# A hybrid encoder step: the small tile moves to the dense expert products, tile 0 to the gathered rows

## Chip, core and metric

The kernel runs on one core of a Trainium2 chip. The metric is the device time of one execution in microseconds; three runs of the kernel before took 3632.94, 3637.1 and 3642.49 us (median 3637.1).

## What is computed

One layer over two streams: a prompt of 1024 frames and a sample of 32 frames with a past of 512. All in float32.

```python
def token_mixer(xn, past_k, past_v, s0, ...):
    z = xn @ w_in                      # 1024 -> 5632
    qa, ka, va, f_pre, q_pre, i_pre, og_pre, gates = jnp.split(z, IN_SPLITS, axis=-1)
    oa = diff_softmax_mix(...)         # 4 heads, two softmax maps, block-causal
    orr, s_new = gla_chunked(...)      # 4 heads, 128x128 state
    y = (jax.nn.sigmoid(ga) * pa + jax.nn.sigmoid(gb) * pb) @ w_out

def peer(xn, w_q, sub_keys, down, up): # 8 heads, 128 x 128 experts of one neuron
    q = (xs @ w_q).reshape(P_TBLOCK, P_HEADS, 2, P_DQ)
    s = jnp.einsum('thcd,hckd->thck', q, sub_keys)
    sv, si = lax.top_k(s, P_TOPK)                      # 16 of 128, twice
    comb = sv[:, :, 0, :, None] + sv[:, :, 1, None, :]
    cv, ci = lax.top_k(comb, P_TOPK)                   # 16 of 256 pairs -> expert e
    gate = jax.nn.softmax(cv, axis=-1)
    hid = jax.nn.gelu(jnp.einsum('thkd,td->thk', down[e], xs), approximate=False)
    return jnp.einsum('thk,thkd->td', gate * hid, up[e])

h = h + token_mixer(rmsnorm(h, norm1))
h = h + peer(rmsnorm(h, norm2))
y = rmsnorm(h, final_norm)
```

Each token uses 8 x 16 = 128 of 16384 experts.

## The kernel before, in words

Tokens lie in nine tiles: 0 to 7 with 128 prompt tokens each, and S with the 32 of the sample. Five generators yield pieces of work with a modelled cost each: `gemm`, `attn`, `routing`, `scatter` and `rows`. A loop at the end of the kernel takes the one that is furthest behind in modelled time; then the framework's scheduler places the instructions on the engines. What results is a fixed order for each engine, and an engine works through its own in order. `issue_after` ties rows and routing to marks of `gemm` (`PACED`).

`gemm` projects the groups of `AG` (`project`), and runs the output stage for the groups of `CDG` (`stage_cd`: gates, w_out, norm, queries, scores). float32 products are three products of split halves (`mm3`). `attn` runs `stage_b` for the groups of `AG`. `routing` finds the 128 experts of a tile (`topk`), in the order `RORDER`.

PEER itself is done in two ways. Tiles in `DENSE` go through all experts: `scatter` writes the gates as a dense matrix to `W_d` with products of one-hot matrices (32 units of four tokens for a full tile, VectorE's `ohB` at line 1138); `hidden(e)` computes gelu of 128 experts for all dense tokens; `gated(e)` multiplies with the gates (line 1217); and `stage_v` multiplies by up-weights and adds into `acc` (line 1280), 32 passes of `jb`, each with four `e`. The tokens are cut into two chunks of `CHUNK` columns. The first `GE` values of `e` are computed before the gates are ready and wait in `early`.

Tiles in `ROWS` gather: for each of a tile's 128 expert places GpSimd issues an indirect DMA of 128 rows of 2048 floats (line 1046), one of three dots is done by GpSimd and ScalarE (1050, 1051) and two by VectorE (1053), ScalarE does gelu and gate (1055, 1056), and VectorE adds the weighted up-row into `xp` (1033). `RB` buffers named `row` turn. Tile S, with 32 tokens, packs four expert places into one gather (32 gathers). A tile's normed input `xg` and its residual `first` come over SP's queue.

Of the kernel before, what the change touches and what calls it, by code (L numbers as in the profile page):

```python
# [9 lines left out]
I32 = mybir.dt.int32  # L10
# [28 lines left out]
RINGS = [(4, 4), (2, 3), (3, 4), (4, 4)]  # L39
SCS = [2, 2, 4, 3]  # L40
# [5 lines left out]
RB, VR, VB, BB, OHB = 5, 3, 2, 4, 4  # L46
# [7 lines left out]
GE = 6  # L54

GC, SC = 1.65, 1.0
# [11 lines left out]
def step_kernel(ctx, tc, x_prompt, x_sample, cache_kT, cache_v, state, norm1, w_in, lam_params,  # L68
# [12 lines left out]
    def open_pool(key, side="left", space=None):  # L81
        kw = dict(space=space) if space is not None else {}
        est[key] = ExitStack()
        P[key] = est[key].enter_context(tc.tile_pool(name=key, bufs=1, side=side, **kw))

# [662 lines left out]
    def stage_cd(ts, rings):  # L748
# [4 lines left out]
        with ExitStack() as st:  # L753
# [99 lines left out]
            def scores(b, qT, keysT):  # L853
                for i, t in enumerate(ts):
# [5 lines left out]
                    pool = P.get("scp") or P.get("oh", wk)  # L860
                    sb = pool.tile([128, 256], F32, name="scs", tag="scs", bufs=SCS[rings])
# [58 lines left out]
    def topk(t):  # L920
        pk, twk = P["pk"], P["twk"]
        T = rows_of(t)
        gate = pk.tile([128, 128], F32, name="gate", tag="gate", bufs=4)
        ei = pk.tile([128, 128], I32, name="ei", tag="ei", bufs=4)
# [3 lines left out]
        if t != "S":  # L928
            ROUTING[t] = (gate, ei)
# [58 lines left out]
        if t == "S":  # L988

            es = pk.tile([128, 32], I32, name="es", tag="es")  # L990
            gs = pk.tile([128, 32], F32, name="gts", tag="gts")
            for g in range(4):
                SP.dma_start(out=es[g * 32:(g + 1) * 32], in_=ei[:32, g * 32:(g + 1) * 32])
                SP.dma_start(out=gs[g * 32:(g + 1) * 32], in_=gate[:32, g * 32:(g + 1) * 32])
            ei, gate = es, gs
        ROUTE[t] = ROUTING[t] = (gate, ei)
# [13 lines left out]
    def rows():  # L1010

        for t in ROWS:
# [3 lines left out]
            T = rows_of(t)  # L1016
            nk = 32 if t == "S" else 128
# [6 lines left out]
            for g in range(128 // T):  # L1024
                SP.dma_start(out=xt[g * T:(g + 1) * T], in_=xn_d[t][:, :])
# [3 lines left out]
            def add(k, row):  # L1029
                if k == 0 and t == "S":  # L1030
                    V.tensor_scalar(acc, row[:, D:], hid[:, 0:1], None, op0=OP.mult)
                else:
                    V.scalar_tensor_tensor(out=acc, in0=row[:, D:], scalar=hid[:, k:k + 1],  # L1033
                                           in1=acc if k else first, op0=OP.mult, op1=OP.add)

            first = None
            if t != "S":
                first = wide("first")[:, 0:D]
                SP.dma_start(out=first, in_=h1_d[t][:, :])

            late = []
            for k in range(nk):
# [15 lines left out]
                yield GC  # L1058
# [3 lines left out]
                yield GC  # L1062
# [3 lines left out]
            sq, fnb, full = hw[:, D:], fw[:, 0:D], fw[:, D:]  # L1066
            SP.dma_start(out=fnb, in_=row_bcast(final_norm))
            ht = acc
            if t == "S":

                ht = hw[:, 0:D]
                SP.dma_start(out=ht[:T], in_=h1_d[t][:, :])
                V.tensor_copy(out=full, in_=acc)
                pw = wide("runs")
                V.tensor_add(ht[:T], ht[:T], acc[:T])
                for g, part in enumerate((pw[:, 0:D], pw[:, D:], sq)):
                    SP.dma_start(out=part[:T], in_=full[(g + 1) * T:(g + 2) * T])
                    V.tensor_add(ht[:T], ht[:T], part[:T])
            normed(gat, ht, fnb, t, sq)
# [3 lines left out]
    NV = 128 * len(DENSE)  # L1083
# [3 lines left out]
    def routing():  # L1087

        for i, t in enumerate(RORDER):
            old = RORDER[i - 4] if i >= 4 else None  # L1090
            while ((t, 0) not in READY or (old in DENSE and old not in DONE)
                   or (t in DEFER and PHASE[0] < 2)):
                yield None
            yield from topk(t)

    def grid(t, s0, q, stg, am, bm):
# [5 lines left out]
        if q + 4 == SB:  # L1102
            o = (128 * DENSE.index(t) + s0) // SB
            SP.dma_start(out=W_d[:, :, o].rearrange("b i j t -> i b j t"), in_=stg)

    def scatter():

        late = None
        for t in [x for ts in CDG for x in ts if x in DENSE]:
# [3 lines left out]
            gate, ei = ROUTE[t]  # L1113
            ij = sct.tile([128, 2, 128], I32, name="ij", tag="ohA", bufs=2)
            V.tensor_scalar(ij[:, 0], ei, 7, None, op0=OP.arith_shift_right)
            V.tensor_scalar(ij[:, 1], ei, 127, None, op0=OP.bitwise_and)
            ijf = sct.tile([128, 2, 128], F32, name="ijf", tag="ohA", bufs=2)
            V.tensor_copy(out=ijf, in_=ij)
            ps = ws_bank()
            for j, src in enumerate((ijf[:, 0], ijf[:, 1], gate)):  # L1120
                PE.transpose(ps[:, j * 128:(j + 1) * 128], src, ident)
            tr = sct.tile([128, 4, 128], F32, name="tr", tag="tr", bufs=1)
            A.activation(tr[:, 0:3], ps.rearrange("p (a t) -> p a t", a=4)[:, 0:3], AF.Copy)
            A.activation(tr[:, 3], ps[:, 0:128], AF.Copy, scale=-1.0)
# [27 lines left out]
    JU, WR = 4, 6  # L1152
# [301 lines left out]
```

## Time and profile before

| | |
|---|---|
| median of three runs | 3637.1 us |
| profiled execution | 3633.46 us |
| its span, first to last instruction | 3631.7 us |
| mean granted TensorE clock | 0.951 |
| TensorE busy | 3261.3 us, 90% |
| VectorE busy | 2795.0 us, 77% |
| ScalarE busy | 1749.2 us, 48% |
| GpSimd busy | 2284.4 us, 63% |

Busy shares are means over stages with different limits, so a table of windows stands among the rows below: its stretches begin where the second attention group's last score products, the output stage's last group, the first gate product, the first product with up-weights, the first accumulate and the 128th accumulate lie. An execution has a fixed part of 1.8 us around the span.

### The profile page before, as it was taken

The page shows a single profiled execution, that of the slowest core. Times are in us where ns is not written, and L with a number is a line of the kernel's source. Part 1 is how long each engine was busy: PE and PEld are TensorE (multiplying, and loading weights), DVE is VectorE, ACT ScalarE, POOL GpSimd, SP SyncE. Part 2 cuts the span into 40 slices and gives each one's busy share as a digit, 9 for nine tenths or more (in the row PEclk, how much of TensorE's full clock was granted, in tenths as well). Part 3 has the DMA queues.
Part 4 walks back from the last instruction along what each step waited for, and adds up shares of the span by engine and source line. Part 5 has one row for each costly group of instructions (what it writes and reads, how often), then busy time and mean ns, then how long its engine had stood idle before and what let it go on. Part 6 is the DMA issues. An engine that isn't in the chain of part 4 may idle for free. (4 is left out here: it accounts for less than half of the span.)

```text
span 3631.7 us, 61063 instructions
## 1 busy us (share of the span) xinstructions
PE 3261.3 (90%) x21635; PEld 3139.3 (86%) x21635; DVE 2795.0 (77%) x5868; ACT 1749.2 (48%) x4314; POOL 2284.4 (63%) x1479
## 2 busy tenths in 40 slices
PE   7999899989898987775888899999999999999997
PEld 7989899878787877775888798999999989999997
DVE  3354468898678989988999998778877788778743
ACT  3544334456777756764443334444444444444432
POOL 2322225546335566686787878888887787888843
PEclk9999999989988999887999999999999999999999
DMA  4554364545555634689788678899988898889842
GB/s 162 166 159 148 118 205 160 161 130 178 177 172 177 216 116 133 204 298 338 283 314 300 247 289 309 331 341 345 335 319 334 308 348 316 327 337 349 321 136 94
DMA packets 357457, 881.05 MB, mean 243 GB/s; under 512 B 31008, under 2 KB 190240, under 8 KB 299808
## 3 DMA queue, kind: packets, MB, share of 16 engines
q1 hardware_dynamic: 297248, 440.91, 36.5%
q0 software_dynamic: 59904, 436.23, 32.2%
q8 instruction: 171, 2.80, 0.3%
q14 instruction: 134, 1.10, 0.1%
HBM read 784.47 MB, written 92.14 MB: 241 GB/s over the span
## 5 line engine op out<-in xcount | busy, mean ns | idle before, releaser
L263 PE MATMUL gv<-vwh,uh 128*128 128x320 f32 x2048 | 644.0, 315 | 105.1 <-DVE acc L1280 67.8
L257 POOL TENSOR_TENSOR wl<-wr,wh 128x1024 fp32r<-128x1024 f32 x160 | 390.4, 2453 | 542.9 <-ACT wh L256 501.9
L263 PE MATMUL gv<-vxh,dh 128*128 128x320 f32 x2048 | 646.1, 316 | 43.7 <-DVE acc L1280 31.1
L265 PE MATMUL gv<-vxh,dl 128*128 128x320 f32 x2048 | 639.9, 314 | 7.3 <-POOL dl L257 7.3
L264 PE MATMUL gv<-vxl,dh 128*128 128x320 f32 x2048 | 641.7, 314 | 0.0
L265 PE MATMUL gv<-vwh,ul 128*128 128x320 f32 x2048 | 635.7, 312 | 4.0 <-POOL ul L257 4.0
L264 PE MATMUL gv<-vwl,uh 128*128 128x320 f32 x2048 | 638.6, 312 | 0.0
L1046 POOL DMA_INDIRECT row<-in_p_rows_dram,ei x384 | 490.6, 1278 | 194.2 <-DVE xp L1033 90.2
L1033 DVE SCALAR_TENSOR_TENSOR xp<-row,hid,xp 128x1024 f32<-128x1024 f32 x412 | 528.1, 1282 | 85.7 <-ACT hid L1056 77.2
L1053 DVE CUSTOM_DVE_ANT_0 row<-row,xg 128x1024 f32<-128x1024 f32 x276 | 507.3, 1838 | 9.3 <-DMA row<-in_p_rows_dram,ei 9.3
L263 PEld LDWEIGHTS gv<-vwh,uh 128*128 128x128 f32 x2048 | 389.0, 190 | 117.9 <-DVE acc L1280 78.5
L263 PEld LDWEIGHTS gv<-vxh,dh 128*128 128x128 f32 x2048 | 394.3, 193 | 50.3 <-issue 32.3
L257 POOL TENSOR_TENSOR ul<-ur,uh 128x512 fp32r<-128x512 f32 x256 | 349.9, 1371 | 131.8 <-ACT uh L256 100.2
L265 PEld LDWEIGHTS gv<-vxh,dl 128*128 128x128 f32 x2048 | 392.5, 192 | 8.6 <-POOL dl L257 8.5
L264 PEld LDWEIGHTS gv<-vxl,dh 128*128 128x128 f32 x2048 | 394.2, 193 | 0.0
L265 PEld LDWEIGHTS gv<-vwh,ul 128*128 128x128 f32 x2048 | 389.1, 190 | 5.1 <-POOL ul L257 5.1
L257 POOL TENSOR_TENSOR dl<-dr,dh 128x512 fp32r<-128x512 f32 x256 | 338.0, 1328 | 86.7 <-ACT dh L256 68.6
L264 PEld LDWEIGHTS gv<-vwl,uh 128*128 128x128 f32 x2048 | 390.0, 190 | 0.0
L1141 POOL TENSOR_TENSOR ohB<-ohB,tr 128x512 f32<-128x512 f32 x160 | 195.4, 1227 | 255.5 <-DVE ohB L1138 216.3
L1050 POOL TENSOR_TENSOR row<-row,xg 128x1024 f32<-128x1024 f32 x140 | 342.3, 2445 | 3.5 <-DMA row<-in_p_rows_dram,ei 2.7
L1280 DVE TENSOR_TENSOR acc<-acc,gv 128x320 f32<-128x320 f32 x496 | 235.3, 480 | 135.9 <-PE gv L265 132.8
L256 ACT ACTIVATE uh<-ur 128x512 fp32r<-128x512 f32 x256 | 160.5, 629 | 231.6 <-PE gv L264 173.0
(327 smaller groups left out, 7812.2 us busy)
## 6 DMA issues: line engine op xcount, KB each, us to landing
dr<-in_p_downT_dram SPq DMA_DIRECT2D x256, 256.0 KB
ur<-in_p_up_dram SPq DMA_DIRECT2D x256, 256.0 KB
wr<-in_w_in_dram SPq DMA_DIRECT2D x88, 512.0 KB
W_d<-stg SPq DMA_DIRECT2D x40, 1024.0 KB
gw<-W_d SPq DMA_DIRECT2D x32, 1280.0 KB
wr<-in_p_wq_dram SPq DMA_DIRECT2D x48, 512.0 KB
wr<-in_w_out_dram SPq DMA_DIRECT2D x24, 512.0 KB
wr<-in_w_a_dram SPq DMA_DIRECT2D x12, 512.0 KB
```

Of the source, the lines that this page charges most:

```text
L256: A.activation(h, src, AF.Copy)
L257: (lo_engine or G).tensor_tensor(out=l, in0=src, in1=h.bitcast(F32), op=OP.subtract)
L263: PE.matmul(out, lh, rh, start=(i == 0), stop=False)
L264: PE.matmul(out, lh, rl, start=False, stop=False)
L265: PE.matmul(out, ll, rh, start=False, stop=(i == n - 1))
L1033: V.scalar_tensor_tensor(out=acc, in0=row[:, D:], scalar=hid[:, k:k + 1], in1=acc if k else first, op0=OP.mult, op1=OP.add)
L1046: G.indirect_dma_start(out=row, out_offset=None, in_=p_rows, in_offset=bass.IndirectOffsetOnAxis(ap=ei[:, k:k + 1], axis=0))
L1050: G.tensor_tensor(out=row[:, 0:D], in0=row[:, 0:D], in1=xt, op=OP.mult)
L1053: V.tensor_tensor_reduce(out=row[:, 0:D], in0=row[:, 0:D], in1=xt, scale=1.0, scalar=0.0, op0=OP.mult, op1=OP.add, accum_out=h)
L1141: G.tensor_tensor(out=bm, in0=bm, op=OP.mult, in1=tr[:, 2, xs].unsqueeze(2).to_broadcast([128, 4, 128]))
L1280: V.tensor_add(acc[:, db, cs], acc[:, db, cs], ps[:, :CHUNK])
```

## The change

S joins the first projection group, the second output group and the dense tiles; tile 0 leaves the dense tiles and is gathered first. A dense tile may now have 32 tokens, so widths come from `VT` and offsets from `VO`. NV falls from 640 to 544. Gathers become 4 x 128 = 512 instead of 3 x 128 + 32 = 416; the packing of four places for S goes. The pools of the gather open at the end of the second attention group instead of at `v_start`; `gemm` waits for that end before the second output group instead of before the third. While `PHASE` is 0 a gather counts 6.6 us of modelled time instead of 3.3. There are four `row` buffers instead of five, eight early values of `e` instead of six, eight buffers for the gated values instead of six, and the scatter's one-hot tiles no longer have a pool of their own with four buffers.

```diff
-AG = [[0, 1, 2, 3, 4], [5, 6, 7, "S"]]
-CDG = [[0, 1, 2], [3, 4], [5, 6, 7, "S"]]
-DENSE = [0, 1, 2, 3, 4]
-ROWS = [5, 6, "S", 7]
-RORDER = [0, 1, 2, 3, 4, 5, 6, 7, "S"]
+AG = [[0, 1, 2, 3, 4, "S"], [5, 6, 7]]
+CDG = [[0, 1, 2], [3, 4, "S"], [5, 6, 7]]
+DENSE = [1, 2, 3, 4, "S"]
+ROWS = [0, 5, 6, 7]
+RORDER = [0, 1, 2, 3, 4, "S", 5, 6, 7]
...
-RINGS = [(4, 4), (2, 3), (3, 4), (4, 4)]
-SCS = [2, 2, 4, 3]
+RINGS = [(4, 4), (2, 3), (3, 3), (4, 4)]
+SCS = [2, 2, 2, 3]
...
+KEPT = dict(d=4, r=3)
-RB, VR, VB, BB, OHB = 5, 3, 2, 4, 4
+RB, VR, VB, BB = 4, 3, 2, 4
-GE = 6
-GC, SC = 1.65, 1.0
+GE = 8
+GC, SC = (3.3, 1.65, 1.65), 1.0
...
-            for k in range(nk):
+            for k in range(128):
...
-                yield GC
+                yield GC[PHASE[0]]
...
-    NV = 128 * len(DENSE)
+    VT = [rows_of(t) for t in DENSE]
+    VO = [sum(VT[:i]) for i in range(len(VT))]
+    NV = sum(VT)
...
-        for i, t in enumerate(RORDER):
-            old = RORDER[i - 4] if i >= 4 else None
-            while ((t, 0) not in READY or (old in DENSE and old not in DONE)
+        for t in RORDER:
+            ts, n = (DENSE, KEPT["d"]) if t in DENSE else (ROWS, KEPT["r"])
+            old = ts[:max(0, ts.index(t) + 1 - n)]
+            while ((t, 0) not in READY or not all(x in DONE for x in old)
...
-            for s0 in range(0, 128, SB):
+            for s0 in range(0, T, SB):
...
-                    pool, bufs = (P["oh"], OHB) if "oh" in P else (sct, 2)
-                    am, bm = [pool.tile([128, 4, 128], F32, name=x, tag=x, bufs=bufs)
+                    am, bm = [sct.tile([128, 4, 128], F32, name=x, tag=x, bufs=2)
...
-    JU, WR = 4, 6
+    JU, WR = 4, 8
...
             ring.close()
+            yield from until("B1")
             with tc.tile_pool(name="scp", bufs=1) as P["scp"]:
...
-            open_pool("oh")
-            yield from until("B1")
             rings("right")
...
-        for key in ("gw", "va", "vk", "vx", "gat"):
+        for key in ("gw", "va", "vk", "vx"):
             open_pool(key, side="right")
-        open_pool("xgp", space=PS)
...
                 yield from stage_b(i)
+            if i == len(AG) - 1 and stop != "mixer":
+
+                open_pool("gat", side="right")
+                open_pool("xgp", side="right", space=PS)
             STATE.add("B%d" % i)
```

How that moves instructions shows at three places. The first is VectorE's order near the end of the dense products, before: `xp` is the sum of a gathered tile, `acc` that of the dense tiles, `msf` the start of a gathered tile's last norm.

```order
L257 TENSOR_TENSOR vwl<-gv,vwh 128x320
L1033 SCALAR_TENSOR_TENSOR xp<-row,hid,xp 128x1024
L1217 TENSOR_TENSOR gv<-gv,gw 128x320
L1033 SCALAR_TENSOR_TENSOR xp<-row,hid,xp 128x1024
L257 TENSOR_TENSOR vwl<-gv,vwh 128x320
L1280 TENSOR_TENSOR acc<-acc,gv 128x320
L240 TENSOR_SCALAR msf<-ssf 128x1
```

The last two row-adds of the last gathered tile stand there, and 48 accumulates and the last gates still follow them. The same engine in the changed kernel, at its last accumulates (`first` is the residual with which a tile's first row-add begins, `ht` the dense tiles' residual):

```order
L1262 TENSOR_TENSOR acc<-acc,gv 128x272
L1024 SCALAR_TENSOR_TENSOR xp<-row,hid,first 128x1024
L1262 TENSOR_TENSOR acc<-acc,gv 128x272
L1224 TENSOR_TENSOR ht<-ht,gv 128x512 x2
L1224 TENSOR_TENSOR ht<-ht,gv 32x512
L1262 TENSOR_TENSOR acc<-acc,gv 128x272 x2
L1042 ISA row,hid<-row,xg 128x1024
L1042 ISA hid 128x1
L1262 TENSOR_TENSOR acc<-acc,gv 128x272 x2
```

Here stands the first row-add of the last gathered tile; 385 of 512 row-adds are placed up to the last accumulate, and 127 after it.

The second place is SP's queue around the load of tile 7's `xg` (`xn_119` is its normed input, `ur` an up-block of the dense products). Before:

```order
L1268 DMA ur<-in_p_up_dram 128x512
L1164 DMA dr<-in_p_downT_dram 128x512
L1268 DMA ur<-in_p_up_dram 128x512
L1025 DMA xg<-xn_119 128x1024
L1164 DMA dr<-in_p_downT_dram 128x512
L1268 DMA ur<-in_p_up_dram 128x512
```

And in the changed kernel:

```order
L1246 DMA fnb<-in_final_norm_dram 128x1024
L1250 DMA ur<-in_p_up_dram 128x512
L1056 DMA fnb<-in_final_norm_dram 128x1024
L1250 DMA ur<-in_p_up_dram 128x512 x2
L1019 DMA xg<-xn_119 128x1024
L1250 DMA ur<-in_p_up_dram 128x512 x2
L1028 DMA first<-h_7_108 128x1024
```

96 up-blocks stood behind that load, and 2 do now.

The third place is TensorE's order at the attention's end (`gb` is an attention product, `ws` one of the scatter, `gm<-act` one of the output stage). Before:

```order
L265 MATMUL gm<-act,wl 128x256
L263 MATMUL gm<-act,wh 128x256
L264 MATMUL gm<-act,wh 128x256
L858 MATMUL gm<-keysT,qT 128x128 x2
L530 MATMUL gb<-ident,on 128x32 x4
L265 MATMUL gm<-act,wl 128x256
```

And in the changed kernel:

```order
L679 MATMUL gb<-ident,kk 128x128 x4
L1081 MATMUL ws<-ohB,ohA 128x128 x4
L685 MATMUL gb<-iv,kkn 128x128 x4
L1081 MATMUL ws<-ohB,ohA 128x128 x8
L536 MATMUL gb<-ident,on 128x128 x4
L1081 MATMUL ws<-ohB,ohA 128x128 x20
L269 MATMUL gm<-act,wh 128x288
```

The attention's last transposes stood among products of the second output group; now that group's first product stands behind them.

## Rows read from the trace of the kernel before

**Rows 1.** the page, engines (instructions) and GB/s moved in 40 slices
```profile
PE 3261.3 (90%) x21635; PEld 3139.3 (86%) x21635; DVE 2795.0 (77%) x5868; ACT 1749.2 (48%) x4314; POOL 2284.4 (63%) x1479
...
GB/s 162 166 159 148 118 205 160 161 130 178 177 172 177 216 116 133 204 298 338 283 314 300 247 289 309 331 341 345 335 319 334 308 348 316 327 337 349 321 136 94
```

**Rows 2.** stretch, us; busy us PE, PEld, DVE, ACT, POOL; clock, DMA share, GB/s
```profile
998.00:1234.00 236.00, 207.56 (x1509) 188.31 (x1510) 191.16 (x535) 176.24 (x447) 108.62 (x68) 0.89 0.61 190
1234.00:1554.00 320.00, 261.99 (x1653) 248.35 (x1653) 301.33 (x844) 205.48 (x495) 188.61 (x117) 0.90 0.49 159
1554.00:1678.00 124.00, 62.03 (x378) 59.50 (x376) 97.50 (x106) 71.51 (x201) 95.24 (x65) 0.72 0.91 331
1678.00:1742.00 64.00, 58.60 (x374) 57.55 (x375) 61.63 (x173) 29.38 (x78) 50.49 (x34) 0.95 0.84 293
1742.00:2278.00 536.00, 467.39 (x2991) 459.21 (x2990) 507.53 (x982) 212.02 (x543) 431.04 (x289) 0.94 0.80 292
2278.00:3611.00 1333.00, 1286.72 (x8664) 1276.73 (x8664) 982.18 (x1391) 562.42 (x1439) 1033.30 (x714) 0.99 0.83 305
3611.00:3632.00 21.00, 1.85 (x17) 1.62 (x15) 11.86 (x24) 3.17 (x10) 6.16 (x5) 0.62 0.32 125
```

**Rows 3.** the same view for the accumulates, line 1280
```profile
2278.00:3611.00 1333.00, 176.09 (x369) 0.99 0.83 305
```

**Rows 4.** the same view for the row-adds, line 1033
```profile
1554.00:1678.00 124.00, 36.27 (x29) 0.72 0.91 331
...
2278.00:3611.00 1333.00, 341.44 (x266) 0.99 0.83 305
3611.00:3632.00 21.00, 0.00 (x0) 0.62 0.32 125
```

**Rows 5.** timeline of TensorE at 320 columns: start, duration, instruction
```profile
2400.31 0.31 PE L265 MATMUL gv<-vxh,dl 128*128 128x320 f32 x1
...
2401.48 0.31 PE L264 MATMUL gv<-vxl,dh 128*128 128x320 f32 x1
```

**Rows 6.** the same view at 256 columns
```profile
60.02 0.28 PE L265 MATMUL gm<-wh,xl 128*128 128x256 f32 x1
...
60.74 0.28 PE L265 MATMUL gm<-wh,xl 128*128 128x256 f32 x1
```

**Rows 7.** groups by line: count | busy us, mean ns | idle before, releasers
```profile
L1033 DVE SCALAR_TENSOR_TENSOR xp<-row,hid,xp 128x1024 f32<-128x1024 f32 x412 | 528.1, 1282 | 85.7 <-ACT hid L1056 77.2 <-issue 2.7 <-ACT hid L1055 2.4
L1053 DVE CUSTOM_DVE_ANT_0 row<-row,xg 128x1024 f32<-128x1024 f32 x276 | 507.3, 1838 | 9.3 <-DMA row<-in_p_rows_dram,ei 9.3
L1046 POOL DMA_INDIRECT row<-in_p_rows_dram,ei x384 | 490.6, 1278 | 194.2 <-DVE xp L1033 90.2 <-issue 31.6 <-DVE si L906 8.1
...
L257 POOL TENSOR_TENSOR ul<-ur,uh 128x512 fp32r<-128x512 f32 x256 | 349.9, 1371 | 131.8 <-ACT uh L256 100.2 <-ACT hid L1055 19.2 <-ACT hid L1056 5.5
L1050 POOL TENSOR_TENSOR row<-row,xg 128x1024 f32<-128x1024 f32 x140 | 342.3, 2445 | 3.5 <-DMA row<-in_p_rows_dram,ei 2.7
L257 POOL TENSOR_TENSOR dl<-dr,dh 128x512 fp32r<-128x512 f32 x256 | 338.0, 1328 | 86.7 <-ACT dh L256 68.6 <-ACT hid L1055 10.3 <-PE gv L265 2.0
...
L969 DVE TENSOR_TENSOR oh<-cf,iota_c 128x800 f32<-128x800 f32 (+1 forms) x72 | 100.1, 1391 | 0.8
...
L974 DVE TENSOR_REDUCE ef<-oh 128x16 f32<-128x800 f32 (+1 forms) x72 | 70.0, 973 | 16.2 <-POOL oh L972 16.2
...
L1053 DVE DVE_READ_ACCUMULATOR2_ANT hid<- 128x1 f32 x276 | 21.6, 78 | 0.0
```

**Rows 8.** busy time by stretch of the scatter's one-hot products, line 1138
```profile
1234.00:1554.00 320.00, 57.42 (x60) 0.90 0.49 159
```

**Rows 9.** the page, GpSimd's DMA queue: packets, MB, share of 16 engines
```profile
q0 software_dynamic: 59904, 436.23, 32.2%
```

**Rows 10.** VectorE's dots, line 1053: min/median/max ns, first and last start
```profile
L1053 DVE CUSTOM_DVE_ANT_0 row<-row,xg x276: 1194/1306/5851, 1533.9 to 3462.4; 128x1024 f32<-128x1024 f32 x138
```

**Rows 11.** waits: who for whom, us in total, times, longest
```profile
POOL row L1046 <- DVE xp L1033: 93.3, 71, 5.6
```

More of the change, by code (lines that the diff above doesn't have):

```diff
@@ L922, in topk @@
         T = rows_of(t)
-        gate = pk.tile([128, 128], F32, name="gate", tag="gate", bufs=4)
-        ei = pk.tile([128, 128], I32, name="ei", tag="ei", bufs=4)
+        kind = "d" if t in DENSE else "r"
+        gate = pk.tile([128, 128], F32, name="gate", tag="gate" + kind, bufs=KEPT[kind])
+        ei = pk.tile([128, 128], I32, name="ei", tag="ei" + kind, bufs=KEPT[kind])
         g3 = gate.rearrange("p (h r) -> p h r", h=PH)
@@ L927, in topk @@
         hg = HG.get(t, PH)
-        if t != "S":
-            ROUTING[t] = (gate, ei)
+        ROUTING[t] = (gate, ei)
         for h0 in range(0, PH, hg):
@@ L987, in topk @@
             yield 1.0
[L988 to L996, printed above, removed]
+        ROUTE[t] = (gate, ei)
         yield 3.0
@@ L1023, in rows @@
             xt = gat.tile([128, D], F32, name="xg", tag="xg", bufs=1)
-            for g in range(128 // T):
-                SP.dma_start(out=xt[g * T:(g + 1) * T], in_=xn_d[t][:, :])
+            SP.dma_start(out=xt, in_=xn_d[t][:, :])
             hid = gat.tile([128, 128], F32, name="hid", tag="hid", bufs=1)
@@ L1029, in add @@
             def add(k, row):
[L1030 to L1039, printed above, removed]
+                V.scalar_tensor_tensor(out=acc, in0=row[:, D:], scalar=hid[:, k:k + 1],
+                                       in1=acc if k else first, op0=OP.mult, op1=OP.add)
+            first = wide("first")[:, 0:D]
+            SP.dma_start(out=first, in_=h1_d[t][:, :])
             late = []
-            for k in range(nk):
+            for k in range(128):
                 while t not in ROUTE and HEADS.get(t, 0) * 16 <= k:
@@ L1065, in rows @@
             hw, fw = wide("ht"), wide("fnb")
-            sq, fnb, full = hw[:, D:], fw[:, 0:D], fw[:, D:]
+            sq, fnb = hw[:, D:], fw[:, 0:D]
             SP.dma_start(out=fnb, in_=row_bcast(final_norm))
[L1068 to L1079, printed above, removed]
+            normed(gat, acc, fnb, t, sq)
+            DONE.add(t)
             yield 4.0
-    NV = 128 * len(DENSE)
+    VT = [rows_of(t) for t in DENSE]
+    VO = [sum(VT[:i]) for i in range(len(VT))]
+    NV = sum(VT)
     SB = 16
@@ L1237, in residual @@
                 cs = slice(d0 * 128, d0 * 128 + 512)
[L1238 removed]
+                for i, (o, T) in enumerate(zip(VO, VT)):
                     ps = gv_bank()
                     for d in range(4):
[L1241 to L1246 removed]
+                        PE.transpose(ps[:T, d * 128:(d + 1) * 128], acc[:, d0 + d, o:o + T], ident)
+                    V.tensor_add(ht[:T, i, cs], ht[:T, i, cs], ps[:T])
+                    A.activation(sq[:T, i, cs], ht[:T, i, cs], AF.Square,
+                                 accum_out=s2[:T, d0 // 4, i:i + 1])
+                    G.tensor_tensor(out=ht[:T, i, cs], in0=ht[:T, i, cs], in1=fnb[:T, cs], op=OP.mult)
             for jb in range(NJ):
@@ L1254, in stage_v @@
                     ss = wk.tile([128, len(DENSE)], F32, name="ss", tag="ss", bufs=1)
[L1255 removed]
+                    V.memset(s2, 1.0)
+                    late = [(ht[:VT[i], i], h1_d[t][:, :]) for i, t in enumerate(DENSE)]
                     late.append((fnb, row_bcast(final_norm)))
@@ L1345, in gemm @@
             yield None
-        for key in ("oh", "sct", "mc"):
+        for key in ("sct", "mc"):
             est[key].close()
@@ L1393, in step_kernel @@
         blocked.clear()
-    for key in ("xgp", "gat", "vx", "vk", "va", "gw", "twk", "pk"):
+    for key in ("xgp", "vx", "vk", "va", "gw", "gat", "twk", "pk"):
         est[key].close()
```

47 lines of the change are left out of this document (21 added, 26 removed).

## The prediction, made before the changed kernel had run

> **What bounds the kernel now.** I read the engine shares first, then busy time by stage, then the spacing of single matmuls, then the groups of VectorE and GpSimd. TensorE is busy 90% of the span [rows 1], but by stage there are two regimes [rows 2]. [...] From 1742 to 2278 us VectorE is busy 507.5 of 536 us: it is the bound, and the first eight passes of the dense products (a pass is one value of `jb`, 16 accumulates) take 67 us each. From 2278 to 3611 us TensorE is the bound: 23 passes (368 accumulates) in 1333 us, 57.96 us each [rows 3]. All 416 gathers are over before the dense products are: the last of the 415 row-adds falls in the stretch that ends at 3611 us, none follows [rows 4], and only 21 us of closing work stand behind the last accumulate.
>
> A matmul of 320 columns starts every 0.146 us (eight steps from 2400.31 to 2401.48) and one of 256 every 0.120 us (six steps from 60.02 to 60.74) [rows 5, 6]. A pass is 384 matmuls of 320 columns, 56.2 us of pure spacing, so it runs at 1.032 of it.
>
> **Dense products.** NV falls from 640 to 544, a chunk from 320 to 272 columns, counts stay. Between the two spacings 272 columns cost 0.120 + 16/64 x 0.026 = 0.1266 us. A pass becomes 384 x 0.1266 = 48.6 us, x 1.032 = 50.2 us. POOL could hold it: in the order 9.9 gathers stand in a pass (228 row-adds over 23 passes; before 266, 11.6 each), so 9.9 x (1.278 + 0.337 x 2.445) + 8 x 1.328 + 8 x 1.371 = 42.4 us [rows 7], 83% of it against 78% before; I add 0.7 us. The 23 passes take 23 x 50.9 = 1170 us, **-163 us**. Ends: 23 x 48.6 (-215) and 57.96 kept (0); I stay near the ratio of the row.
>
> First eight passes: in the order VectorE has 28 row-adds fewer between accumulates 1 and 128 (77 against 105) at 1.282 + 2/3 x 1.916 = 2.56 us (-72 us), 46 us less routing (tile 6's is ahead of it now), and 9 us less from narrower gates and accumulates. Its 507.5 us become 380, at the same 95% 400 us. TensorE asks 8 x 50.2 = 402 us. Two engines at the limit take turns badly, so 425 us instead of 536, **-111 us** (ends -136 and -40).
>
> **Up to the first accumulate.** Tile 0's gathers now stand among routing and scatter. Ahead of its first accumulate VectorE's order has 80 row-adds instead of 44 (36 x 1.282 = +46 us), 54 dots instead of 30 (24 x 1.916 = +46 us), 136 one-hot products instead of 160 (24 x 0.957 = -23 us) [rows 7, 8], and routing for six heads more, some 27 us (their two one-hot steps alone are 6 x (1.391 + 0.973) = 14 us). That is +96 us on an engine busy 88% of 744 us. Also, the attention's end is now waited for ahead of the second group of the output stage: in TensorE's order 172 attention matmuls and 119 of the scatter stand alone, where before nearly all of the attention's last 305 lay among the output stage's (a stretch of TensorE's order only; what they take alone no row shows). Dense work queues behind it. If VectorE stays 88% busy the first accumulate is 96/0.88 = 109 us later; if its 92 us of idle time take up the gathers, 0; if the lone attention adds idle time like the 45 of 236 us that VectorE has there now [rows 2], or somewhat more, 170. I take **+105 us**: where gathers meet routing VectorE is busy 94 to 96% [rows 2], so there is little left to fill.
>
> Moved edits that I cost at nothing: S goes from the second projection group to the first (columns 640 + 416 become 672 + 384, three chunks both times); its outputs come from the dense stage instead of regrouped gathers (32 gathers less, which are in the counts above); eight gelu columns instead of six wait ahead of the gates, hidden beside the scatter as now. If that cover is gone, two columns are 96 matmuls, 12 us.
>
> **The tail.** Here the order decides. In VectorE's order 415 of 415 row-adds stood ahead of the last accumulates; now 385 of 512 do, and 127 follow, all of tile 7. SP's queue loads tile 7's `xg` with two up-blocks left behind it, where 96 were left before, so no dot of it can start earlier. Nothing is left beside them: each gather of 128 rows x 8 KiB = 1.049 MB is exposed. Price of one: GpSimd's queue moved 436.23 MB in 32.2% of sixteen engines' span, 436.23/(0.322 x 3631.7 us) = 373 GB/s, 2.81 us [rows 9]. VectorE alone, at the dot's median 1.306 us [rows 10]: 1.282 + 2/3 x (1.306 + 0.077) = 2.20 us. Above: 29 row-adds in the 124 us from 1554 to 1678 [rows 4], 4.3 us, with scatter, weights and hidden columns beside them. I take 3.0 us, near the queue's price, since four buffers keep the transfers back to back: 127 x 3.0 = 381 us (279 to 546). Behind the last add stands one norm and one store, some 13 us, instead of the 21 us of now: **+373 us**.
>
> [...]
>
> **Sum.** The profiled execution took 3633.46 us (span 3631.7). 3633.5 + 105 - 111 - 163 + 373 = 3837.5 us. The median of the runs is 3.6 us above that execution: 3840 us.
>
> **Rivals.**
> *The scatter sets the start (other side).* The gates wait for the last scatter unit; 24 units fewer at 320/60 = 5.3 us each [rows 8] would bring the dense start 128 us forward instead of 105 back: 3837 - 233 = 3604 us. For it: 92 us of idle VectorE there. Against: VectorE works in order and has 96 us more. It decides only if the first accumulate comes before about 1650 us. 4%.
> *VectorE paces the tail.* 127 x 2.20 = 279 us: 3735 us. Against: the queue's price is above that. 12%.
> *The tail is latency.* With four buffers instead of five each gather waits for its predecessor's add: 4.3 us, 546 us: 4003 us. For it: GpSimd waited 93.3 us for row-adds [rows 11]. 10%.
> *Passes don't shorten.* GpSimd's splits queue behind gathers that wait for one of four buffers, a pass stays 57.96 us: 3837 + 163 = 4000 us. Against: POOL's 42 us fit in 50. 8%.
> *The change doesn't do what it says* can be read off: tile 0 does start early (59 of its row-adds ahead of the first gate), yet the dense end is reached with 385 done where the earlier start was to leave fewer. That is in the forecast.
>
> **Chances.** Forecast 66%, its own range 3760 to 3920 us. Range for 8 in 10: 3700 to 3960 us, which takes in VectorE's tail and leaves out most of the three others. Under 0.3% (11 us) this kernel's runs can't tell from none. Faster 4% (the scatter rival), same 2% (a mixture of it with a fast tail), slower 94%.
>
> **What would show it.** Right: TensorE idle for the last 350 to 420 us, with row-adds as VectorE's main work and one queue at some 350 GB/s; last accumulate near 3445 us; first near 1847 us; passes near 51 us; TensorE's low share also between attention's end and the second group's first product. Wrong: row-adds of tile 7 beside dense matmuls; a last accumulate above 3550 us or a first below 1742 us; a gather above 3.6 us in the tail.

## The result, and the profile after

The changed kernel takes 3908.3 us (median of 4 runs, 3899.4 to 3909.2) against 3636.4 us of the kernel before: ratio 1.074, 95% interval 1.0719 to 1.0762. The forecast was 3840 us, its range 3700 to 3960 us. Line numbers are now those of the changed kernel: row-add L1024, dot L1042, gather L1035, accumulate L1262.

The page of the changed kernel, answering to [rows 1, 9]: the engines' busy time, TensorE's busy tenths and granted clock in 40 slices, GpSimd's DMA queue.

```profile
PE 3039.0 (78%) x21443; PEld 2908.2 (74%) x21443; DVE 2904.9 (74%) x6064; ACT 1759.4 (45%) x4428; POOL 2443.5 (63%) x1583
...
PE   7999979998756568767788999999999999960000
...
PEclk9999989989878679878899999999999999985555
...
q0 software_dynamic: 73728, 536.90, 36.7%
```

TensorE has nothing to do in the last four slices, and the queue carries 100.7 MB more: the 96 added gathers. The stages, in the columns of [rows 2]:

```profile
990.00:1133.00 143.00, 89.93 (x516) 74.77 (x514) 76.07 (x169) 96.22 (x263) 40.04 (x35) 0.77 0.50 156
1133.00:1306.00 173.00, 105.71 (x674) 97.74 (x674) 135.29 (x153) 90.24 (x234) 103.44 (x68) 0.80 0.81 280
1306.00:1538.00 232.00, 165.92 (x985) 155.65 (x985) 220.09 (x723) 86.71 (x173) 129.99 (x66) 0.82 0.63 225
1538.00:1758.00 220.00, 152.24 (x889) 144.12 (x889) 198.78 (x554) 146.57 (x358) 143.50 (x89) 0.83 0.44 139
1758.00:1887.00 129.00, 89.53 (x603) 84.76 (x601) 83.04 (x90) 89.50 (x245) 83.12 (x63) 0.80 0.69 233
1887.00:1939.00 52.00, 45.65 (x310) 44.26 (x311) 48.96 (x141) 21.23 (x60) 30.95 (x24) 0.88 0.81 292
1939.00:2378.00 439.00, 397.41 (x3025) 392.36 (x3025) 409.06 (x832) 181.81 (x467) 353.26 (x245) 0.96 0.79 285
2378.00:3490.00 1112.00, 1091.11 (x8605) 1085.65 (x8603) 855.71 (x1289) 510.11 (x1330) 954.36 (x667) 0.99 0.89 328
3490.00:3897.00 407.00, 1.23 (x10) 0.78 (x8) 272.61 (x318) 112.33 (x350) 266.25 (x171) 0.50 0.86 324
```

From 990 us (last projection matmul) to 1133 us (the second output group's first product) TensorE is busy 63%, all of it attention and scatter. The first accumulate starts at 1939 us, the last at 3490 us, and 407 us without TensorE follow. The same view for the row-adds alone:

```profile
3490.00:3897.00 407.00, 162.49 (x127) 0.50 0.86 324
```

The 127 row-adds stand in the tail as the order said, 407/127 = 3.2 us each. Span against span the 275 us divide as follows, in us:

| part | before | after | measured | forecast |
|---|---|---|---|---|
| start to first accumulate | 1742 | 1939 | +197 | +105 |
| first eight passes | 536 | 439 | -97 | -111 |
| 23 later passes | 1333 | 1112 | -221 | -163 |
| behind the last accumulate | 21 | 417 | +396 | +373 |

A piece of the tail's timeline (start, duration, engine, line; in brackets the idle time before and who ended it):

```profile
3703.74 0.94 POOL L1035 DMA_INDIRECT row<-in_p_rows_dram,ei  x1 [1.19 <-DVE xp L1024]
3704.77 1.22 DVE L1042 CUSTOM_DVE_ANT_0 row<-row,xg 128x1024 f32<-128x1024 f32 x1
...
3706.59 1.29 DVE L1024 SCALAR_TENSOR_TENSOR xp<-row,hid,xp 128x1024 f32<-128x1024 f32 x1 [0.60 <-ACT hid L1045]
...
3710.87 1.23 DVE L1042 CUSTOM_DVE_ANT_0 row<-row,xg 128x1024 f32<-128x1024 f32 x1 [2.99 <-DMA row<-in_p_rows_dram,ei]
...
3713.57 0.95 POOL L1035 DMA_INDIRECT row<-in_p_rows_dram,ei  x1 [2.93 <-DVE xp L1024]
```

Two waits face each other: VectorE's dot waits 2.99 us for a row to land, and GpSimd's next gather waits 1.19 to 2.93 us for a row-add to free a buffer. Which of them sets the 3.2 us, the timeline can't say.

### The profile page after: what moved, and what is told of

The parts are those of the page before. It is cut to its first block, busy times and chain, and to the rows that moved or that the text cites. A ratio compares the mean times of both kernels' runs of the same rounds, so it can differ in the third digit from the quotient of the medians.

```text
span 3906.7 us, 61161 instructions
## 1 busy us (share of the span) xinstructions
PE 3039.0 (78%) x21443; PEld 2908.2 (74%) x21443; DVE 2904.9 (74%) x6064; ACT 1759.4 (45%) x4428; POOL 2443.5 (63%) x1583
## 4 chain that ended last, share of the span: by engine, by line
PE 36%; DVE 24%; POOL 8%; issue 7%; DMA 7%; ACT 4%; POOLq 0%; SPq 0%; DVEq 0%; ACTq 0%
PE gv L271 9%; PE gv L269 9%; PE gv L270 8%; DVE xp L1024 5%; POOL row L1039 3%; DMA row<-in_p_rows_dram,ei 3%; DVE row L1042 3%; POOL row L1035 3%; PE gm L270 2%; PE gm L269 2%; PE gm L271 2%; PE ws L1081 2%; DVE oh L974 1%; DVE ohB L1120 1%; ACT row L1040 1%
## 5 line engine op out<-in xcount | busy, mean ns | idle before, releaser
L1035 POOL DMA_INDIRECT row<-in_p_rows_dram,ei x512 | 652.5, 1274 | 322.2 <-DVE xp L1024 184.6
L1024 DVE SCALAR_TENSOR_TENSOR xp<-row,hid,xp 128x1024 f32<-128x1024 f32 x508 | 652.1, 1284 | 133.1 <-ACT hid L1045 121.1
L1042 DVE CUSTOM_DVE_ANT_0 row<-row,xg 128x1024 f32<-128x1024 f32 x340 | 582.7, 1714 | 128.6 <-DMA row<-in_p_rows_dram,ei 128.3
L269 PE MATMUL gv<-vxh,dh 128*128 128x272 f32 x2048 | 598.4, 293 | 45.9 <-DVE vwl L263 20.2
L269 PE MATMUL gv<-vwh,uh 128*128 128x272 f32 x2048 | 593.8, 290 | 23.9 <-DMA ur<-in_p_up_dram 12.5
L271 PE MATMUL gv<-vxh,dl 128*128 128x272 f32 x2048 | 596.6, 294 | 13.7 <-POOL dl L263 13.4
L270 PE MATMUL gv<-vxl,dh 128*128 128x272 f32 x2048 | 595.7, 292 | 0.0
L271 PE MATMUL gv<-vwh,ul 128*128 128x272 f32 x2048 | 589.4, 290 | 4.9 <-POOL ul L263 4.8
L270 PE MATMUL gv<-vwl,uh 128*128 128x272 f32 x2048 | 592.7, 290 | 0.0
L1044 ACT ACTIVATE hid<-hid 128x1 f32<-128x1 f32 x512 | 100.5, 198 | 573.5 <-DVE hid L1042 566.8
L1040 ACT ACTIVATE row<-row 128x1024 f32<-128x1024 f32 x172 | 181.9, 1057 | 315.2 <-POOL row L1039 312.3
```

What stands on the lines that cost most here:

```text
L269: PE.matmul(out, lh, rh, start=(i == 0), stop=False)
L270: PE.matmul(out, lh, rl, start=False, stop=False)
L271: PE.matmul(out, ll, rh, start=False, stop=(i == n - 1))
L1035: G.indirect_dma_start(out=row, out_offset=None, in_=p_rows, in_offset=bass.IndirectOffsetOnAxis(ap=ei[:, k:k + 1], axis=0))
L1040: A.activation(row[:, 0:D], row[:, 0:D], AF.Copy, accum_out=h)
L1042: V.tensor_tensor_reduce(out=row[:, 0:D], in0=row[:, 0:D], in1=xt, scale=1.0, scalar=0.0, op0=OP.mult, op1=OP.add, accum_out=h)
```

## The experiments

A time below is that of a single run unless an interval stands beside it.

### The start: lone attention or gathers

First the kernel before, in which the loop that orders the work issues the second output group behind the attention's last TensorE instruction:

```diff
+            yield from until("B1")
+            CDF[0] = 1
+            yield 0.0
             with tc.tile_pool(name="scp", bufs=1) as P["scp"]:
...
+        if x[0] == "gemm" and CDF[0] and tails:
+            hold = tails[-1]
```

> The kernel before, whole and with its own tiles and gathers, with one edit: the second output group's instructions are issued only behind the attention's last TensorE instruction, so that 190 attention and 115 scatter matmuls stand alone ahead of it in TensorE's order (172 and 119 in the changed kernel, 13 and 16 in the kernel before). Theory (the lone attention is part of the late start): the 123 us that the changed kernel's trace shows between the last projection matmul and the second group's first product, less what still overlaps, come back here: first accumulate 80 to 130 us later than 1742 us, total 3715 to 3765 us. Rival (VectorE's added gathers alone make the start late, and the attention only changes places): first accumulate within 30 us of 1742 us, total 3630 to 3665 us.

The first accumulate came at 1829 us, 87 us later, and the run took 3732.6 us against 3648.7 us of the kernel before beside it. Its stretch from the last projection matmul to the attention's end:

```profile
979.00:1120.00 141.00, 108.91 (x537) 80.58 (x537) 83.48 (x208) 97.84 (x293) 36.91 (x30) 0.67 0.46 135
```

141 us, as the changed kernel's 143 (the 123 us of the expectation are a misreading); VectorE is busy 59% of them. The theory holds: the lone attention alone is worth 84 to 87 us in the kernel before.

Then both kernels without the gathers but each tile's first:

```diff
+                if k and True:
+                    yield GC[PHASE[0]]
+                    yield GC[PHASE[0]]
+                    continue
                 row = wide("row")
```

> The changed kernel without 127 of the 128 gathers of each of tiles 0, 5, 6 and 7 (508 of 512, with their dots and row-adds; the output of these four tiles is left incomplete); every other instruction keeps its place. Theory: 79 of them stood ahead of the first accumulate, 79 x 2.56 us of VectorE at its 88% there is 230 us, so the first accumulate comes near 1710 us; what is left above the same kernel before without gathers is the lone attention. The tail vanishes: nothing but closing work of some 20 us behind the last accumulate. TensorE holds the passes at 47 to 48.5 us in both dense stretches, total 1710 + 31 x 47.7 + 20 = 3210 us. Rival 1 (the lone attention and the scatter make all of the late start, the gathers lay in idle time): first accumulate at 1850 us or later. Rival 2 (gathers, not TensorE, pace the passes even late): passes below 46 us.

> The kernel before without the gathers but the first of each of its tiles 5, 6, 7 and S (412 of 416 left out with their dots and row-adds; these tiles' output is left incomplete). The partner of the run above: the first accumulate should come 43 x 2.56 / 0.88 = 125 us sooner, near 1617 us; passes stay near 57.5 us, in the first eight too, total 1617 + 31 x 57.6 + 21 = 3424 us. The two first accumulates' distance is what the change adds ahead of the dense work without gathers: the theory of the lone attention gives 80 to 130 us, the theory that gathers alone explain the +197 us gives under 30 us.

The dense stages, of the changed kernel without gathers and then of the kernel before without them (first accumulate to accumulate 128, and to the last):

```profile
1775.00:2152.00 377.00, 375.11 (x2983) 374.19 (x2982) 193.94 (x619) 130.40 (x263) 190.29 (x141) 1.00 0.37 123
2152.00:3239.00 1087.00, 1087.00 (x8668) 1086.95 (x8667) 327.29 (x758) 361.00 (x727) 473.16 (x364) 1.00 0.35 115
```

```profile
1674.00:2131.00 457.00, 447.21 (x3007) 444.15 (x3006) 220.46 (x676) 135.93 (x264) 200.54 (x146) 0.99 0.32 105
2131.00:3420.00 1289.00, 1274.92 (x8658) 1268.17 (x8657) 368.10 (x777) 365.40 (x729) 472.77 (x364) 1.00 0.31 100
```

The first accumulates are 1775 and 1674 us, 101 us apart without a gather. So of the +197 us the new structure ahead of the dense work makes 101 and the gathers 96. Of the 101, the lone attention accounts for 87 if it costs here what it cost in the kernel before; 10 already lie ahead of the last projection matmul, which comes at 991 us against 981. The gathers cost 164 us for 79 now and 68 us for 43 before. A gather there costs 2.1 and 1.6 us, less than the 2.9 us I had put into both expectations, which is why both first accumulates come 57 to 65 us later than I wrote. TensorE alone needs 1087/23 = 47.3 us for a pass, and 48.3 us with gathers: it is the bound there, as forecast.

The two whole runs say what the change is worth by itself: 3264.7 us against 3442.9 us, so without gathers the changed kernel is 178 us the faster one. Its 508 left-out gathers, with their dots and row-adds, cost 644 us; the 412 of the kernel before cost 194 us.

### The tail: who sets 3.2 us

The changed kernel with tile 7's places cut into stretches:

```diff
+                m = 64 if t == 7 and k >= 80 else 128
...
+                if t == 7 and (56 <= k < 80 or k >= 104):
+                    A.activation(h, gate[:m, k:k + 1], AF.Copy)
+                elif k % RP == 1 and not (t == 7 and 32 <= k < 56):
```

> The changed kernel with tile 7's 128 places cut in five stretches: places 0 to 31 as they are; 32 to 55 with all dots on VectorE and none on GpSimd; 56 to 79 with no dot at all, only the row-add (the dots are left out); 80 to 103 as they are but with 64 rows in each gather instead of 128; 104 to 127 with 64 rows and no dots (tile 7's output is left wrong). Spacing of row-adds in the five, us each. Theory (the transfers' bytes pace the tail): 3.2, 3.2, 3.2, then 1.6 to 2.2 (VectorE's own work takes over), then 1.6; total some 60 us below 3907 us. Rival 1 (each gather's latency over four buffers): 3.2, 3.2, about 3.0, 2.9 to 3.2, 2.9, total within 25 us of 3907 us. Rival 2 (GpSimd's queue, in which a gather is issued behind a multiply that waits for its row): 3.2, 2.7, below 2.5, 3.0, below 2.0. Rival 3 (VectorE paces): 3.2, then 2.7 to 3.2, then 1.3.

Row-adds (VectorE's busy time and their count) from one row-add's start to another's, well inside each of the five stretches; then clock, DMA share, GB/s:

```profile
3499.90:3590.53 90.63, 33.42 (x26) 0.50 0.90 333
3608.34:3666.01 57.67, 23.18 (x18) 0.50 0.92 341
3679.21:3724.84 45.63, 23.18 (x18) 0.50 1.01 421
3747.52:3812.24 64.72, 23.03 (x18) 0.50 0.68 146
3826.56:3875.51 48.95, 24.32 (x19) 0.50 1.02 206
```

Width by count: 3.49, 3.20, 2.54, 3.60 and 2.58 us; the run took 3887.2 us. None of the four theories fits. With all dots on VectorE the pace is 3.20 us, and the changed kernel takes 3.22 us at those places, so the multiplies on GpSimd don't set it. Without dots the sixteen DMA engines are full (share 1.01) and a gather takes 2.5 us; half the rows take as long. So I split the question anew: a fixed latency over the buffers, or a full queue, and ran two kernels on it, one with more row buffers and one with fewer (the last two lines of the diff are the second kernel's).

```diff
+                    open_pool("tl")
+                if t == 7 and k >= 32 and (k < 80 or k % 5 > 1):
+                    row = P["tl"].tile([128, 2 * D], F32, name="row", tag="row", bufs=6)
...
-RB, VR, VB, BB = 4, 3, 2, 4
+RB, VR, VB, BB = 3, 3, 2, 4
```

> The changed kernel; tile 7's places 0 to 31 gather into the four row buffers as they are, from place 32 on into a second pool of six buffers (opened when the dense stage has left its memory), from place 80 on into both in turn, ten buffers. Places 64 to 79 and 104 to 127 have no dot, only the row-add (tile 7's output is left wrong by those). Spacing of the row-adds, us each, for 4 buffers, 6 with dots, 6 without, 10 with, 10 without. Theory A (a gather takes some 8.6 us from issue to use whatever its bytes, as the equal 2.49 and 2.56 us for 128 and 64 rows suggest, so four buffers set the pace): 3.2 to 3.5, 2.3 to 2.7, 1.7, 2.2 to 2.4 (VectorE's own work), 1.3; total 3775 to 3810 us. Theory B (the queue carries 421 GB/s and is full, so bytes set the floor and buffers don't matter): 3.2 to 3.5, 2.7 to 3.2, 2.5, 2.5 to 3.0, 2.5; total 3840 to 3880 us.

> The same five stretches of tile 7 as in the run with stretches before (as is; all dots on VectorE; no dots; 64 rows; 64 rows and no dots, the output of tile 7 left wrong), but with three row buffers instead of four in the whole kernel; 141 row-adds instead of 127 stand behind the last accumulate. Theory A (latency over the buffers): 4.2 to 4.7, 4.0, (8.6 + 1.5) / 3 = 3.4, 4.2 to 4.8, 3.4. Theory B (bytes): as with four, 3.5, 3.0, 2.5, at most 3.6, 2.5. The dense passes beside fewer gathers stay within 1 us of 48.3 us in both.

The same view, for 4 buffers with dots, 6 with, 6 without, 10 with, 10 without:

```profile
3526.93:3621.92 94.99, 33.46 (x26) 0.50 0.91 358
3635.29:3709.98 74.69, 33.49 (x26) 0.50 0.97 382
3719.62:3744.51 24.89, 12.88 (x10) 0.50 1.01 420
3759.75:3805.11 45.36, 23.17 (x18) 0.50 1.01 422
3816.09:3858.63 42.54, 24.49 (x19) 0.50 0.95 393
```

That is 3.65, 2.87, 2.49, 2.52 and 2.24 us (the last stretch began with rows that had landed). With three buffers, first as is, then without dots, then with 64 rows and no dots:

```profile
3664.08:3764.82 100.74, 33.46 (x26) 0.50 0.75 268
...
3866.46:3914.14 47.68, 23.19 (x18) 0.50 0.98 395
...
4032.11:4081.06 48.95, 24.32 (x19) 0.50 1.01 206
```

3.87, 2.65 and 2.58 us. The pace also changes with the place in the tail, so here is the changed kernel with its four buffers, at the places of the three stretches with dots (4, 6 and 10 buffers):

```profile
3506.82:3594.87 88.05, 33.47 (x26) 0.50 0.90 340
3613.23:3694.80 81.57, 33.50 (x26) 0.50 0.89 335
3765.45:3820.16 54.71, 23.20 (x18) 0.50 0.91 343
```

3.39, 3.14 and 3.04 us. The latency theory wanted 3.4 us without dots at three buffers and 1.3 at ten: it falls. Without dots a gather takes 2.5 to 2.65 us with three, four and six buffers, at a DMA share of 0.98 to 1.01 (the full-queue theory, but not by its bytes: 64 rows should then have been quicker). With dots the pace quickens with each buffer added, compared at the same places: 3.87 us with three and 3.39 to 3.65 with four; 3.14 with four and 2.87 with six; 3.04 with four and 2.52 with ten. With dots, four buffers do not keep the queue full (share 0.89 to 0.92 in these stretches, against 1.01 without dots); a buffer is held while dot, gelu and row-add follow each other, and GpSimd's next gather waits up to 2.93 us for that row-add in the timeline above. By these rows the change's own step from five buffers to four adds to its tail, but no run has five there. The kernels took 3870.7 and 4092.7 us. I missed the passes with three buffers: 1185/23 = 51.5 us, not 48.3; what in them waits longer was not shown.

### Where else could the gathers stand

Ahead of the dense work: the changed kernel without due times for the gathers.

```diff
-PACED = dict(rows=(1, 2), routing=(0, 1, 2))
+PACED = dict(rows=(), routing=(0, 1, 2))
```

> The changed kernel, whole, but the gathers are no longer held back to their due times in the order: 167 row-adds instead of 80 stand ahead of the first accumulate, 475 instead of 385 ahead of the last, 37 instead of 127 behind it. Theory (a gather ahead of the dense work costs 164/79 = 2.1 us, as the two runs without gathers show, one in the tail 3.2 us): first accumulate 1939 + 87 x 2.1 = 2120 us, last near 3670, tail 37 x 3.2 = 118 us, total 3770 to 3830 us. Rival 1 (the gathers fill idle time ahead of the dense work): first accumulate before 2030 us, total near 3710 us. Rival 2 (VectorE's total work decides, so it doesn't matter where a gather stands): total 3885 to 3930 us.

3829.1 us; first accumulate 2141 us, last 3691 us:

```profile
1131.00:2141.00 1010.00, 605.79 (x3434) 567.19 (x3435) 909.77 (x1878) 512.33 (x1304) 672.60 (x423) 0.75 0.75 266
...
3691.00:3817.00 126.00, 1.38 (x13) 1.06 (x11) 87.81 (x108) 35.00 (x109) 81.16 (x53) 0.52 0.84 313
```

87 gathers moved ahead cost 202 us, 2.3 each, with VectorE 90% busy; 90 fewer behind save 417 - 136 = 281 us, 3.1 each. The theory holds at its upper end.

Beside the passes: the order makes room for 13 gathers in each.

```diff
+        if x[0] == "gemm" and PHASE[0] == 2:
+            hold = next((m for v, m in reversed(radds) if v <= x[2] - 0.0), None)
```

> The changed kernel, whole; only the order of the dense stage is changed: each piece of it is issued behind the row-adds that were due before it, so that some 13 gathers instead of 9.9 stand in a pass (171 row-adds instead of 157 ahead of accumulate 128, 474 instead of 385 ahead of the last, 38 instead of 127 behind it). Theory (the order and not an engine left the gathers for the tail; beside TensorE-bound passes a gather is nearly free, 48.3 us with 9.9 of them against 47.9 without): VectorE gets 15.4 + 13.2 x 2.2 = 44 us and GpSimd 48 us of work in a pass, so passes of 49.5 to 51.5 us, tail 38 x 3.2 + 10 = 132 us, total 3660 to 3720 us. Rival (the late passes had no room: GpSimd or VectorE was the bound at 9.9 already): passes of 54 to 58 us, total 3760 to 3860 us.

3949.3 us, slower than the change itself. The later passes, and what TensorE waited for in them (us in total, times, longest):

```profile
2433.00:3801.00 1368.00, 1163.45 (x8674) 1150.76 (x8672) 1009.30 (x1460) 569.79 (x1535) 1095.22 (x765) 0.92 0.88 323
```

```profile
PE gv L269 <- ACT vwh L262: 146.1, 37, 12.3
PE gv L269 <- DVE acc L1262: 28.8, 15, 6.1
```

A pass takes 1368/23 = 59.5 us (without gathers 47.3, not the expectation's 47.9). The theory falls, and by more than the rival said. VectorE and GpSimd are busy 74 and 80%, so neither is full; TensorE waits for ScalarE's splits of the gated values, up to 12.3 us at a time. Its granted clock is 0.92 over the stretch: it is busy 1163 us with 8674 matmuls, where 8668 took 1087 us at 1.00 in the run without gathers. So 76 of the 281 us between these two stretches, about a quarter, are longer busy time for as many matmuls, at the lower clock; that the waits lower the clock was not shown. DMA stands at 323 GB/s, near that of the other stretches full of gathers (323 to 329), so I suspected the bytes and halved them:

```diff
-                G.indirect_dma_start(out=row, out_offset=None, in_=p_rows,
+                G.indirect_dma_start(out=row[:, 0:D], out_offset=None,
+                                     in_=p_rows.rearrange("e (t d) -> (e t) d", t=2),
```

> The kernel with 13 gathers in a pass again (473 row-adds ahead of the last accumulate), but each gather fetches rows of 4 KiB instead of 8 KiB; dot and row-add read the same half, so that VectorE, ScalarE and GpSimd do as much as before (the output of the four gathered tiles is left wrong). Theory (the DMA rate is the bound: in every stretch with gathers it stands at 323 to 329 GB/s, and a pass moves some 5.4 MB of weights and gates and 1.049 MB for each gather, so 13.2 of them take 59 us): with half rows a pass moves 12.3 MB, 38 us of DMA, and falls back to TensorE's 48 to 50.5 us; total 3580 to 3660 us. Rival (VectorE, ScalarE and GpSimd wait for each other in the queues that now hold 13 gathers a pass): passes stay at 57 to 60 us, total above 3850 us.

The same stretch, and what TensorE waited for in nearly all of it (2365 to 3630 us):

```profile
2359.00:3642.00 1283.00, 1145.48 (x8662) 1116.85 (x8661) 1083.65 (x1462) 542.57 (x1519) 1110.35 (x766) 0.97 0.66 218
```

```profile
PE gv L271 <- POOL dl L263: 50.4, 50, 2.4
PE gv L271 <- POOL ul L263: 26.5, 17, 6.3
PE gv L269 <- DVE vwl L263: 25.8, 12, 5.2
```

1283/23 = 55.8 us a pass, 3789.6 us in all: between the two. Of the 11.2 us that a pass had grown, half the bytes take back 3.7; with the DMA engines a third free (share 0.66), TensorE waits for splits on GpSimd and VectorE, whose queues now hold gather work between them. Which of these waits would be the last to go isn't settled. In its tail the last row-adds stand 3.2 us apart, though each gather moves half the bytes (164 GB/s, share 0.49): there too the bytes do not set the pace.

### The kernel before with other places for its gathers

Without gathers its dense work starts 68 us sooner, so I moved them from there into the passes, in three kernels: from the fifth pass on, from the third pass on (15 in a pass), and with one condition only, that the gates are done. The first two also issue the dense work behind the row-adds that were due before it and give GpSimd every fourth dot instead of every third. The edit of the third, whole:

```diff
-            while t not in ROUTING or "gat" not in P:
+            while t not in ROUTING or "gat" not in P or PHASE[0] < 2:
```

> The kernel before, whole, with its own tiles and columns, but its 416 gathers are moved out of the stages that VectorE bounds and into the passes that TensorE bounds: none stands ahead of the first accumulate (44 before), 57 in the first eight passes (105 before) and some 15.4 in each later pass (11.6 before); every fourth dot on GpSimd instead of every third. Theory (a gather costs where VectorE is the bound and is nearly free beside TensorE-bound passes, as the runs without gathers show): first accumulate near 1680 us as without gathers (1674), first eight passes 470 to 500 us instead of 536, later passes 58 to 61 us instead of 58, total 3540 to 3600 us: faster than both kernels. Rival (15.4 gathers a pass are too many for VectorE and GpSimd): later passes 63 us or more, total 3630 us or above.

> As the run before it, with the gathers from the third pass on: none ahead of the first accumulate, 92 in the first eight passes, 15 a pass for the next sixteen, fewer at the end. Theory: first accumulate near 1680 us, first eight passes 500 to 530 us, later ones 57.5 to 60 us, total 3545 to 3605 us, within 15 us of the run before. Rival: as there, 3630 us or above.

> The kernel before, whole, with one condition more: the gathers begin only when the gates are done, so that 24 row-adds stand ahead of the first accumulate instead of 44, 104 (105) follow in the first eight passes, and 12.5 instead of 11.6 in each later pass. Theory (the DMA rate allows (57.9 x 0.325 - 5.5) / 1.049 = 12.7 gathers beside a pass of 58 us, so 20 can be moved there for nothing from where VectorE pays 1.6 us for each): first accumulate 1742 - 20 x 1.6 = 1710 us, later passes 58 to 59 us, total 3600 to 3630 us, faster than both kernels. Rival (late passes lose what the start gains): total 3632 to 3660 us.

The first took 3705.0 us (ratio 1.0186, interval 1.0169 to 1.0203), the second 3643.2 us: the start came at 1670 and 1668 us as expected, but the later passes took 66.2 us with 15.3 gathers and 62.5 us with 14.1. The rival was right. The third, which moves 20 gathers, took 3604.1 us: ratio 0.9899, interval 0.9882 to 0.9915, 1% faster than the kernel before. Its first accumulate came at 1716 us and its passes took 57.9 us, as its theory said; but the theory's reason, a DMA rate that leaves room for 12.7 gathers, was argued only; with half the bytes a pass of the changed kernel got back 3.7 of 11.2 us. The later passes of the first and the third:

```profile
2141.00:3663.00 1522.00, 1341.37 (x8677) 1320.11 (x8677) 1207.47 (x1657) 600.00 (x1610) 1166.58 (x801) 0.94 0.88 329
```

```profile
2249.00:3581.00 1332.00, 1283.83 (x8658) 1272.95 (x8657) 1050.24 (x1440) 577.21 (x1494) 1075.69 (x744) 0.99 0.87 323
```

Read together, a pass of 640 columns takes 56.0 us without gathers and 58.0, 57.9, 62.5 and 66.2 us with 11.6, 12.5, 14.1 and 15.3: nearly free up to about 12.5, then some 3 us each. A pass of 544 columns takes 47.3, 48.3 and 59.5 us with none, 10 and 13.2: if the slope is the same, an estimate, it is full at 9 to 10. The changed kernel was near that point already.

Two things keep this from being shown as a matter of the count alone. The kernels with 13.2, 14.1 and 15.3 gathers in a pass also issue their dense work behind row-adds. And divided the other way, each gather takes 4.3 to 4.5 us in these three and in the one with half rows, as it would if the gather loop had a pace of its own there, as in the tail. No run has more row buffers beside the passes.

## Why the prediction was right, and where it was not

Of its signs, TensorE without work at the end (407 us) and row-adds as VectorE's work there came, and none of the signs of being wrong. But the terms are not all right.

**The tail (+373, measured +396).** Place and count were right, and the price nearly (3.2 for 3.0 us), by luck: "four buffers keep the transfers back to back" fails, for the full queue gives 2.5 us and more buffers approach it. It is the rival *the tail is latency* in kind, with buffers held, at 3.2 instead of 4.3 us; *VectorE paces the tail* falls, since the pace changes with the buffers while VectorE's work stays.

**"Here the order decides."** Only half true. The order said where the gathers fall, and an order that puts all but 37 ahead of the last accumulate by moving them in front of the dense work saves 79 us. But one that puts all but 38 there by moving them into the passes is 41 us slower than the change, and neither comes near the kernel before. The count weighs more: 96 gathers more, and all gathers together cost 644 us instead of 194. That the shorter passes hold 10 instead of 12.5 of them, and that each one without a place there costs 2.1 to 3.2 us, fits the runs; it is read from pass times and not shown by itself.

**Up to the first accumulate (+105, measured +197).** This is the step that failed. The kernel before, from its last projection matmul to where [rows 2] go on:

```profile
976.00:998.00 22.00, 14.90 (x65) 9.25 (x62) 20.75 (x46) 19.21 (x50) 10.42 (x6) 0.77 0.90 286
```

From the last projection matmul to the first accumulate VectorE works 672 of 766 us there, and 762 of 949 us in the changed kernel. Its work grew by 90 us, near the +96 of the order; its idle time grew by 93 us, where the forecast had some 10, its "88% busy" (651.6 of 744 us [rows 2]) being 80%. The remaining 14 us lie ahead of that matmul, where S's projection has moved, which I had put at nothing; that has no run of its own. (That the runs without gathers also give +96 for the gathers is chance: each cost less than the forecast's 2.9 us, and each more in the changed kernel than before.) I took the lone attention as idle time that this work might fill or that might raise the term a little, at most to 170; by itself it cost 84 to 87 us in the kernel before. That nothing fills it can be read from the stretch: VectorE is busy 76 of its 143 us in the changed kernel, and as little, 77 of 138 us, in the kernel without gathers. Gathers could not fill it, for the change opens their buffers only at the attention's end: the first is issued at 1110 us, behind the attention's last matmul at 1104. The rival *the scatter sets the start* was right that the dense work begins behind the last scatter matmul (1874 and 1887 us, before 1651 and 1678), but that matmul came 224 us later and not 128 us sooner.

**The 23 later passes (-163, measured -221).** The mechanism was right, TensorE the bound, and the size off. Two matmuls of 272 columns in the changed kernel, twelve steps apart:

```profile
2900.00 0.29 PE L269 MATMUL gv<-vxh,dh 128*128 128x272 f32 x1
...
2901.50 0.29 PE L269 MATMUL gv<-vxh,dh 128*128 128x272 f32 x1
```

0.125 us each, not 0.1266, so 48.0 us for 384 of them; and the factor for what a pass loses beside that was 1.007, not the 1.032 that I carried over from [rows 3] with 0.7 us on top. Spacing, factor and surcharge make 0.6, 1.2 and 0.7 of the 2.5 us by which I had a pass too long. The 384 are themselves too many: the last pass has no hidden products of a next one, and 8664 matmuls in 23 passes [rows 2] are 377 each. That is 47.1 us at 0.125, as the run without gathers shows (47.3), so a pass really loses 1.2 us now and lost 2.9 before. *Passes don't shorten* did not happen.

**The first eight passes (-111, measured -97).** Right in kind: VectorE is the bound, busy 409 of 439 us, though with 409 us of work instead of 380. TensorE was not at its limit as I had it (402 us): without gathers these passes take 377 us, so 77 gathers cost 62 us there. That two engines at their limit take turns badly was my estimate; no run shows it.

The errors at the start and in the later passes, +92 and -58 us, partly cancel; with +14 and +23 they give the 71 us between 3838 and 3908 us. So the total owes its nearness in part to luck.

## What to carry to other kernels

Work that rides beside a bound stage may find room for only so many items in each step, and here the shorter step seemed to have room for fewer: count the items that lose their place and price them at the rate of the exposed loop before counting the stage's gain. A step that is moved to stand alone is a term of the sum by itself, not idle time for others to fill, unless the same trace shows who would fill it. When a ring of buffers and a queue wait for each other in a trace, only a run with other buffer counts tells which one sets the pace, and it has to be compared at the same place of the loop.

## What the runs showed of the hardware

A gather of 64 rows of 8 KiB took as long as one of 128: 2.58 against 2.54 us, at 206 and 421 GB/s with the DMA engines' share at 1.02 and 1.01; with three buffers instead of four 64 rows took 2.58 us again. All gathers of 64 rows here wrote to the first 64 partitions; no run used other partitions, so why half the rows take as long was not shown.

The 323 to 329 GB/s that all stretches of passes full of gathers share look like a limit, but with half the gathers' bytes the passes were only 6% shorter, at 218 GB/s. Bytes are therefore not what makes most of such a pass; whether 329 GB/s is a ceiling of this mixed load no run settles, and the 421 GB/s of a tail without dots are above it. And TensorE's granted clock stood at 0.50 through the tail, where it issued ten matmuls in 407 us.
